# A two-layer hybrid trunk on one core: branch and output blocks as 512+256-column chains, with a written order on ScalarE and VectorE

## The chip, the cores and the metric

The kernel runs on one core of one Trainium2 chip. The metric is the device time of one execution in microseconds, the median of three runs: 999.44 us before (999.4 to 999.6). The profile is of one execution of the same program.

The engines are named as in the profile: PE is TensorE's matmuls and PEld its weight loads, DVE is VectorE, ACT is ScalarE, POOL is GpSimd, SP is SyncE, whose queue issues nearly all DMAs.

## The reference

Sequence 256, width 1024, two layers. All arithmetic is float32. One layer, cut to what matters:

```python
x = x + 0.5 * swiglu(rms_norm(x, ffn1_norm), ffn1_w_gate_up, ffn1_w_down)
z = rms_norm(x, mix_norm) @ w_in            # u (512), q, k, v (512 each), gate logits (2 x 1024)
y_pool = multiscale_pool(u, pool_w, pool_scale)     # trailing means over 2/4/8/16 positions
y_attn = moba_attention(rope(norm(q)), rope(norm(k)), v)   # one block of 256: causal attention
gates  = sigmoid(gl + b_gate)                       # 2 x 1024
merged = gates[0] * (y_pool @ w_branch_pool) + gates[1] * (y_attn @ w_branch_attn)
x = x + merged @ w_out
x = x + 0.5 * swiglu(rms_norm(x, ffn2_norm), ffn2_w_gate_up, ffn2_w_down)
```

## The kernel before

**Exact products from split operands.** Every float32 operand of a large matmul is held as two parts, high and low. A product of weights and activations is three terms: high weights by high activations, high by low, low by high. Activations lie as `[128, 2, 256]`: 256 columns of the high part, then 256 of the low part. `chain` (line 140) makes the three terms in two matmuls: the high weights against all 512 columns (both parts at once, into two halves of a PSUM tile), then the low weights against the 256 high columns, added to the first half. The two halves of the PSUM tile must be added afterwards. `chain3` (line 145) makes them in three matmuls of 256 columns, all into one half, so that nothing has to be added. Below, a *block* is one 128x128 weight block with its three terms; a *pair* is a block by `chain`, a *triple* a block by `chain3`.

**Weights.** They come in units of 16 blocks (1 MB): one DMA on SP into `raw` (four buffers), then for each of two halves a copy on ACT (`hi<-raw`, line 122) and a subtraction on DVE (`lo<-raw,hi`, line 123), each over 128x1024. `hi` and `lo` have six halves each, three units. `request` issues one unit's DMA and its two splits; `unit` takes the next one. `raw` comes free when DVE has made the low part, and only then can SP issue the DMA that waits for it.

**The order.** `mm` and whatever stands in `keep(...)` stays in the order in which it is written; the other instructions on ACT, DVE and POOL are placed among them by a list scheduler of the tile framework. Each engine runs its own list strictly in order.

**The stages of a layer.** FFN 1 (gate-up units, then down projection), then `mix`: q, k, v, u, the gates and attention interleaved, then the branch stage and the output stage, then FFN 2.

**Branch stage** (lines 737 to 780). For each of eight output blocks f there are 4 blocks of pooling (`pk`) and 4 of attention (`yk`): 64 blocks in a layer, four units. f = 2, 3 and 4 (`wide`) are pairs, whose halves are added by ACT and DVE (lines 756 and 757); the other five are triples. The first four f are done in two passes over k. `mixed(f)` multiplies by the two gates (line 758), adds the two products (line 759, on POOL for wide f) and splits the sum into `mk[f]` (`halves`: ACT line 205, DVE line 206).

**Output stage** (`project`, lines 783 to 804). For each f there are 8 blocks of `mk`: 64 in a layer, four units. f < 4 are pairs: ACT copies the second half to `t`, POOL adds x (line 799), DVE adds the first half (line 800). f >= 4 are triples with one addition on DVE. Then `after(f)`, which is `prep`: the new x is scaled and split into `hx[f]` for FFN 2 (ACT line 251, DVE line 252), squared and accumulated (lines 260 and 261).

**What waits there.** The output stage's first chains read `mk[0]` to `mk[5]` and only later `mk[6]`, `mk[7]`. FFN 2 begins with unit 0 over `hx[0]` to `hx[6]`, unit 1 over `hx[0]`, `hx[1]`, then `hx[7]`; after a few more blocks comes the sum of squares over the partitions, two matmuls `ss<-ar,one_r`, where `ar` is the split of `acc` and needs the last square.

Of the kernel before, what the change touches and what calls it, by code (L numbers as in the profile page):

```python
# [49 lines left out]
def trunk_kernel(ctx: ExitStack, tc: tile.TileContext, x_in, w_in, pw_in, qkn_in, rope_in, mask_in, band_in, out):  # L50
# [182 lines left out]
    nc.gpsimd.memset(uT[:, :, :PAD], 0.0)  # L233
# [8 lines left out]
    keep(nc.gpsimd.dma_start(gx[:, L * NG + 2 * S:L * NG + 4 * S], x_in[:, L * NG + 2 * S:L * NG + 4 * S]))  # L242

# [19 lines left out]
    def prep(f, l, col):  # L263
        split_x(f, l, col)
        square_x(f)
# [300 lines left out]
    def mix(l, after):  # L566
# [26 lines left out]
        def open_gate(f):  # L593
            tt(gates[:, f], gates[:, f], bc2(r), op=OP.mult)
            for j in range(2):
                c = j * NK + f
                act(gates[:, f, j, :], gates[:, f, j, :], AF.Tanh, scale=0.5, bias=hb[:, c:c + 1])
# [142 lines left out]
        def branch(f, j, k0=0, k1=4):  # L740
            if f not in sums:
                sums[f] = quarter("two")
            if f in wide:
                for k in range(k0, k1):
                    chain(sums[f][j], *ws[f // 2], f % 2 * 8 + j * 4 + k, (pk, yk)[j][k], k == 0, k == 3)
            else:
                chain3(sums[f][:, j], *ws[f // 2], f % 2 * 8 + j * 4 + k0, (pk, yk)[j][k0:k1], k0 == j == 0,
                       j == 1 and k1 == 4)

        def mixed(f):  # L750
            mg = tmp.tile([P, 2, S], F32, name="mg", tag="t512", bufs=5)
            both = sums[f]
            if f in wide:
                both = mg
                for i in range(2):
                    act(mg[:, i, :], sums[f][i][:, 1, :], AF.Copy)
                    tt(mg[:, i, :], sums[f][i][:, 0, :], mg[:, i, :], op=OP.add)
            stt(mg, gates[:, f], 1.0, both, op0=OP.add, op1=OP.mult)
            (nc.gpsimd.tensor_tensor if f in wide else tt)(mg[:, 0, :], mg[:, 0, :], mg[:, 1, :], op=OP.add)
            halves(mk[f], mg[:, 0, :])  # L760

        ws = [unit() for _ in range(2)]
        sums = {f: quarter("two") for f in range(2)}
        wide = range(2, 5)
        sums.update({f: banks(pmm, "two") for f in range(2, 4)})
        sums = {f: [z[:, j] for j in range(2)] if f in wide else z for f, z in sums.items()}
        sums[4] = [quarter("two") for _ in range(2)]
        for f in range(4):
            for j in range(2):
                branch(f, j, 0, 2)  # L770
        for f in range(4):
            for j in range(2):
                branch(f, j, 2)
            mixed(f)
        for f in range(4, NK):
            if f % 2 == 0:
                ws.append(unit())
            for j in range(2):
                branch(f, j)
            mixed(f)  # L780
        ws, sums = [], []

        def project(f, k0=0, k1=NK):
# [5 lines left out]
            if f >= 4:  # L789
                chain3(ps[:, 0], *ws[f // 2], f % 2 * 8 + k0, mk[k0:k1], k0 == 0, k1 == NK)  # L790
            else:
                for k in range(k0, k1):
                    chain(ps, *ws[f // 2], f % 2 * 8 + k, mk[k], k == 0, k == NK - 1)
            if k1 == NK:
                t = x[:, f, :]
                if f < 4:
                    t = small.tile([P, S], F32, name="t", tag="sg", bufs=2)
                    act(t, ps[:, 1, :], AF.Copy)
                    nc.gpsimd.tensor_tensor(t, t, x[:, f, :], op=OP.add)
# [135 lines left out]
```

## Time and profile before

| | |
|---|---|
| median of three runs | 999.44 us |
| profiled execution, its own time | 999.57 us |
| its span | 997.6 us |
| PE busy | 993.6 us, 100% of the span |
| DVE busy | 799.5 us, 80% |
| ACT busy | 628.7 us, 63% |
| POOL busy | 17.5 us, 2% |
| granted TensorE clock | 1.0 throughout |
| branch stage of layer 1, layer 2 | begins at 280.00 us and 774.11 us |
| output stage | begins at 301.90 us and 796.00 us |
| FFN 2 | begins at 323.59 us and 817.70 us |

A row of the timeline gives start, duration, engine, line, operation, tiles, shapes and count; equal instructions that follow each other are one row. The records of neighbouring instructions overlap: a matmul's record is longer than the distance to the next one's start. So rates are read from start to start. Groups give busy time, mean duration of one, and the idle time before them with what ended it.

### The profile page before, as it was taken

Reading aid. Unit: us, or ns where it says so; the run is one execution under the profiler, and the core shown is the slowest. Engines: PE = TensorE matmul, PEld = TensorE weight load, DVE = VectorE, ACT = ScalarE, POOL = GpSimd, SP = SyncE. Lnnn points to the kernel's source line nnn. Section 1 sums busy time; section 2 is a strip of 40 time slices with the busy share of each in tenths; the row PEclk is TensorE's granted clock in tenths of the full one; section 3 lists DMA queues with packets and bytes.
Section 4 is the critical chain, followed back from the end, with each engine's and each line's share of the span. In section 5 each row is a group of like instructions: output and inputs, shape, how many; then the busy total and the mean of one; then the engine's idle time right before and its main releaser. Section 6 shows DMA issues by size and latency. Waiting matters only on the chain.

```text
span 997.6 us, 15761 instructions
## 1 busy us (share of the span) xinstructions
PE 993.6 (100%) x6220; PEld 899.1 (90%) x6220; DVE 799.5 (80%) x1183; ACT 628.7 (63%) x999; POOL 17.5 (2%) x53
## 2 busy tenths in 40 slices
PE   9999999999999999999999999999999999999998
PEld 8998888898899988988898898888989999889888
DVE  7987786799879988886688888667998799888752
ACT  7766565657866766655576666556678567656541
POOL 1000000000001000000000000000000010000000
PEclk9999999999999999999999999999999999999999
DMA  9655565643536655655556566555545266555640
GB/s 314 243 207 209 194 245 214 220 170 120 219 127 211 214 208 182 204 207 204 181 193 215 178 211 205 182 204 191 193 151 194 100 235 216 198 204 189 211 143 27
DMA packets 30154, 192.88 MB, mean 193 GB/s; under 512 B 3360, under 2 KB 5408, under 8 KB 7552
## 3 DMA queue, kind: packets, MB, share of 16 engines
q1 hardware_dynamic: 29664, 191.18, 55.0%
q8 instruction: 48, 0.79, 0.3%
q0 software_dynamic: 128, 0.39, 0.1%
q10 hardware_dynamic: 288, 0.31, 0.1%
q14 instruction: 26, 0.21, 0.1%
HBM read 190.82 MB, written 1.05 MB: 192 GB/s over the span
## 4 chain that ended last, share of the span: by engine, by line
PE 100%; DVE 0%; issue 0%
PE ps L80 85%; PE pt L80 6%; PE two L80 4%; PE at L80 2%; PE pe L80 1%; PE at L546 1%; PE busy L80 0%; PE tp L507 0%; PE ss L80 0%; DVE gx L451 0%
## 5 line engine op out<-in xcount | busy, mean ns | idle before, releaser
L80 PE MATMUL ps<-hx,hi 128*128 128x512 f32 (+1 forms) x1714 | 572.2, 383 | 0.0
L123 DVE TENSOR_TENSOR lo<-raw,hi 128x1024 fp32r<-128x1024 f32 (+2 forms) x333 | 393.9, 1189 | 115.3 <-ACT hi L122 110.6
L80 PE MATMUL ps<-hx,lo 128*128 128x256 f32 x1712 | 464.6, 273 | 0.0
L122 ACT ACTIVATE hi<-raw 128x1024 fp32r<-128x1024 f32 (+2 forms) x333 | 339.6, 1029 | 190.4 <-PE ps L80 153.9
L80 PEld LDWEIGHTS ps<-hx,hi 128*128 128x128 f32 x1714 | 321.1, 188 | 56.8 <-issue 0.3
L80 PEld LDWEIGHTS ps<-hx,lo 128*128 128x128 f32 x1712 | 321.2, 188 | 0.8
L80 PE MATMUL ps<-ga,hi 128*128 128x512 f32 (+1 forms) x264 | 87.0, 376 | 0.0
L80 PE MATMUL ps<-gc,hi 128*128 128x512 f32 (+1 forms) x264 | 87.0, 376 | 0.0
L80 PE MATMUL ps<-ga,lo 128*128 128x256 f32 x256 | 69.9, 273 | 0.0
L80 PE MATMUL ps<-gc,lo 128*128 128x256 f32 x256 | 69.9, 273 | 0.0
L80 PE MATMUL ps<-gb,hi 128*128 128x512 f32 (+1 forms) x198 | 65.6, 376 | 0.0
L80 PE MATMUL pt<-hi,hx 128*128 128x512 f32 x192 | 64.3, 382 | 0.0
L80 PEld LDWEIGHTS ps<-ga,hi 128*128 128x128 f32 x264 | 49.0, 188 | 8.3
L80 PEld LDWEIGHTS ps<-gc,hi 128*128 128x128 f32 x264 | 49.0, 188 | 8.3
L80 PE MATMUL pt<-lo,hx 128*128 128x256 f32 x192 | 52.5, 273 | 0.0
L80 PE MATMUL ps<-gb,lo 128*128 128x256 f32 x192 | 52.4, 273 | 0.0
L190 DVE TENSOR_TENSOR ab<-ps,ab 128x512 f32<-128x512 f32 x56 | 38.6, 688 | 16.2 <-ACT ab L189 14.9
L80 PEld LDWEIGHTS ps<-ga,lo 128*128 128x128 f32 x256 | 48.1, 188 | 0.0
L80 PEld LDWEIGHTS ps<-gc,lo 128*128 128x128 f32 x256 | 48.1, 188 | 0.0
L388 DVE TENSOR_TENSOR lo<-raw,hi 128x1024 fp32r<-128x1024 f32 x38 | 44.7, 1217 | 0.0
L80 PE MATMUL two<-yp,hi 128*128 128x256 f32 (+1 forms) x208 | 43.9, 301 | 0.0
L80 PE MATMUL ps<-mk,hi 128*128 128x256 f32 (+1 forms) x192 | 43.5, 311 | 0.0
(162 smaller groups left out, 1130.1 us busy)
## 6 DMA issues: line engine op xcount, KB each, us to landing
raw<-w SPq DMA_DIRECT2D x176, 1024.0 KB, 4.9
raw<-w SPq DMA_DIRECT2D x6, 256.0 KB, 6.0
raw<-w SPq DMA_DIRECT2D x11, 128.0 KB, 3.8
raw<-w SPq DMA_DIRECT2D x2, 512.0 KB, 6.1
gx<-x SPq DMA_DIRECT2D x2, 256.0 KB, 5.7
qk<-pw SPq DMA_DIRECT2D x2, 256.0 KB, 3.3
out_dram<-gx SPq DMA_DIRECT2D x2, 256.0 KB, 2.7
out_dram<-gx SPq DMA_DIRECT2D x1, 384.0 KB, 5.4
```

Source lines behind the costliest of these rows:

```text
L80: return keep(nc.tensor.matmul(*args, **kw))
L122: put(act(hi, w, AF.Copy))
L123: put(tt(lo, w, hi.bitcast(F32), op=OP.subtract))
L190: put(tt(t, ps[:, :, 0, :], t, op=OP.add))
L388: keep(tt(lo[h], raw[:, h * HALF:(h + 1) * HALF], hi[h].bitcast(F32), op=OP.subtract))
L546: keep(nc.tensor.transpose(line(pt)[:, j * P:(j + 1) * P], pr[:, h, c * P:(c + 1) * P], ident))
```

## The change

- **Branch stage.** All eight f are pairs, one f after the other, each with its own PSUM tile (four single tiles by turns with the double ones). `mixed(f)` for each: two ACT copies, two additions, the gate product, the sum on DVE (none on POOL), `halves`. `mk[f - 1]` is split after f's gate product.
- **Gate 7.** Its sums are drained where they were, after three requests, but `open_gate(7)` (times r on DVE, two Tanh on ACT) stands behind f = 3.
- **Output stage.** All eight f are pairs: `t` copied by ACT, then two additions on DVE, none on POOL.
- **Weights.** `next_half` makes half a unit at a time at written places: after f = 0, 1, 2, 4 and 6 of the branches, three after the last, one after each of f = 0 to 5 of the output, two at the end.
- **Order.** All of these, and the `prep` behind the output stage, are in `keep`.
- **Padding.** The 16 zero columns of `uT` are cleared by 16 memsets of one column each, after POOL's DMA of x, in place of one memset before it.

```diff
-    nc.gpsimd.memset(uT[:, :, :PAD], 0.0)
...
     keep(nc.gpsimd.dma_start(gx[:, L * NG + 2 * S:L * NG + 4 * S], x_in[:, L * NG + 2 * S:L * NG + 4 * S]))
+    for t in range(PAD):
+        keep(nc.gpsimd.memset(uT[:, :, t:t + 1], 0.0))
...
-        gate(7)
-        open_gate(7)
+        last = sum_pair(unit())
+        for _ in range(3):
+            request()
+        drain(gates[:, 7], last, keep)
...
+        def next_half():
+            if not begun:
+                raw = raws.tile([P, 2 * HALF], F32, name="raw", tag="raw")
+                nc.sync.dma_start(raw, w_in[n_unit[0]])
+                n_unit[0] += 1
+                begun.append((raw, [], []))
+            raw, hi, lo = begun[0]
+            h = len(hi)
...
+            split(raw[:, h * HALF:(h + 1) * HALF], hi[h], lo[h], keep)
+            if h:
+                begun.clear()
+                ahead.append((hi, lo))
...
-            (nc.gpsimd.tensor_tensor if f in wide else tt)(mg[:, 0, :], mg[:, 0, :], mg[:, 1, :], op=OP.add)
-            halves(mk[f], mg[:, 0, :])
...
+        def mixed(f, ps):
+            mg = tmp.tile([P, 2, S], F32, name="mg", tag="t512", bufs=5)
             for j in range(2):
+                keep(act(mg[:, j, :], ps[j][:, 1, :], AF.Copy))
             for j in range(2):
+                keep(tt(mg[:, j, :], ps[j][:, 0, :], mg[:, j, :], op=OP.add))
+            keep(stt(mg, gates[:, f], 1.0, mg, op0=OP.add, op1=OP.mult))
+            return mg
...
+        for f in range(NK):
             if f % 2 == 0:
                 ws.append(unit())
+                ps = [quarter("two") for _ in range(2)]
+            else:
+                ps = banks(pmm, "two")
+                ps = [ps[:, j] for j in range(2)]
             for j in range(2):
+                for k in range(4):
+                    chain(ps[j], *ws[f // 2], f % 2 * 8 + j * 4 + k, (pk, yk)[j][k], k == 0, k == 3)
+            mgs.append(mixed(f, ps))
+            if f:
+                halves(mk[f - 1], mgs[f - 1][:, 0, :], keep)
+            keep(tt(mgs[f][:, 0, :], mgs[f][:, 0, :], mgs[f][:, 1, :], op=OP.add))
+            if f == 3:
+                open_gate(7, keep)
+            if f in (0, 1, 2, 4, 6):
+                next_half()
+        halves(mk[-1], mgs[-1][:, 0, :], keep)
+        for _ in range(3):
+            next_half()
...
-            if f >= 4:
-                chain3(ps[:, 0], *ws[f // 2], f % 2 * 8 + k0, mk[k0:k1], k0 == 0, k1 == NK)
...
             if k1 == NK:
-                    nc.gpsimd.tensor_tensor(t, t, x[:, f, :], op=OP.add)
-                tt(x[:, f, :], ps[:, 0, :], t, op=OP.add)
+                t = small.tile([P, S], F32, name="t", tag="sg", bufs=2)
+                keep(act(t, ps[:, 1, :], AF.Copy))
+                keep(tt(x[:, f, :], ps[:, 0, :], x[:, f, :], op=OP.add))
+                keep(tt(x[:, f, :], x[:, f, :], t, op=OP.add))
+                if f < 6:
+                    next_half()
                 after(f)
...
+        for _ in range(2):
+            next_half()
```

ACT's list in layer 1, from the drain of gate 7 to the copy for f = 4 (`gates<-gates,hb` is the Tanh, `mg<-two` the copy of a wide sum's second half), before:

```order
L189 ACTIVATE gates<-ps 128x512
L597 ACTIVATE gates<-gates,hb 128x256 x2
L122 ACTIVATE hi<-raw 128x1024
L205 ACTIVATE mk<-mg 128x256
L122 ACTIVATE hi<-raw 128x1024 x2
L756 ACTIVATE mg<-two 128x256
```

ACT's list in the change, from the copies for f = 2 to those for f = 4:

```order
L764 ACTIVATE mg<-two 128x256 x2
L205 ACTIVATE mk<-mg 128x256
L122 ACTIVATE hi<-raw 128x1024
L764 ACTIVATE mg<-two 128x256 x2
L205 ACTIVATE mk<-mg 128x256
L598 ACTIVATE gates<-gates,hb 128x256 x2
L764 ACTIVATE mg<-two 128x256 x2
```

The two Tanh of gate 7 moved from ahead of the branches to between the copies for f = 3 and f = 4.

DVE's list in layer 1 for one f of the branch stage and the gate product that follows f = 3, before (f = 1 and 2, as the scheduler mixed them):

```order
L758 SCALAR_TENSOR_TENSOR mg<-gates,two 128x512
L123 TENSOR_TENSOR lo<-raw,hi 128x1024
L759 TENSOR_TENSOR mg<-mg 128x256
L757 TENSOR_TENSOR mg<-two,mg 128x256
L123 TENSOR_TENSOR lo<-raw,hi 128x1024
L206 TENSOR_TENSOR mk<-mg,mk 128x256
```

DVE's list in the change, f = 3 and the beginning of f = 4:

```order
L766 TENSOR_TENSOR mg<-two,mg 128x256 x2
L767 SCALAR_TENSOR_TENSOR mg<-gates,mg 128x512
L206 TENSOR_TENSOR mk<-mg,mk 128x256
L784 TENSOR_TENSOR mg<-mg 128x256
L595 TENSOR_TENSOR gates<-gates,r 128x512
L766 TENSOR_TENSOR mg<-two,mg 128x256 x2
L767 SCALAR_TENSOR_TENSOR mg<-gates,mg 128x512
```

Every f has now two additions `mg<-two,mg`, and the sum `mg<-mg` is always DVE's.

DVE's list in layer 1 at the end of the output stage (`gx` holds x), f = 4 and 5 before:

```order
L800 TENSOR_TENSOR gx<-ps,gx 128x256 x2
L123 TENSOR_TENSOR lo<-raw,hi 128x1024
L252 SCALAR_TENSOR_TENSOR hx<-gx,hx 128x256
L261 TENSOR_TENSOR acc<-acc,sq 128x256
L252 SCALAR_TENSOR_TENSOR hx<-gx,hx 128x256
L261 TENSOR_TENSOR acc<-acc,sq 128x256
```

The same place in the change, f = 4 and the beginning of f = 5:

```order
L805 TENSOR_TENSOR gx<-ps,gx 128x256
L806 TENSOR_TENSOR gx<-gx,t 128x256
L123 TENSOR_TENSOR lo<-raw,hi 128x1024
L253 SCALAR_TENSOR_TENSOR hx<-gx,hx 128x256
L262 TENSOR_TENSOR acc<-acc,sq 128x256
L805 TENSOR_TENSOR gx<-ps,gx 128x256
L806 TENSOR_TENSOR gx<-gx,t 128x256
```

Each f has one more addition, and half a weight unit stands between the new x and its split in each f up to 5.

More of the change, by code (lines that the diff above doesn't have):

```diff
@@ L591, in gate, with open_gate @@
             pair(unit(), gates[:, f], *other)
[L593 to L594 removed]
+        def open_gate(f, put=lambda i: i):
+            put(tt(gates[:, f], gates[:, f], bc2(r), op=OP.mult))
             for j in range(2):
                 c = j * NK + f
[L597 removed]
+                put(act(gates[:, f, j, :], gates[:, f, j, :], AF.Tanh, scale=0.5, bias=hb[:, c:c + 1]))
         def project_u():
@@ L734, in mix @@
             map_end(2 + p, ats[2 + p])
-        gate(7)
-        open_gate(7)
+        last = sum_pair(unit())
+        for _ in range(3):
+            request()
+        drain(gates[:, 7], last, keep)
         mt = acts.tile([P, NK, 2, S], F32R, name="mk", tag="ga")
         mk = [mt[:, i] for i in range(NK)]
[L740 to L748, printed above, removed]
@@ L750, in mixed @@
-        def mixed(f):
-            mg = tmp.tile([P, 2, S], F32, name="mg", tag="t512", bufs=5)
[L752 to L759, printed above, removed]
-            halves(mk[f], mg[:, 0, :])
@@ L762, in mix @@
[L762 to L768, printed above, removed]
+        begun = []
+        def next_half():
[6 more added lines that the diff above has]
+            h = len(hi)
+            hi.append(parts.tile([P, HALF], F32R, name="hi", tag="hi"))
+            lo.append(parts.tile([P, HALF], F32R, name="lo", tag="lo"))
+            split(raw[:, h * HALF:(h + 1) * HALF], hi[h], lo[h], keep)
+            if h:
+                begun.clear()
+                ahead.append((hi, lo))
@@ L788, in project @@
             ps = sums[f]
-            if f >= 4:
-                chain3(ps[:, 0], *ws[f // 2], f % 2 * 8 + k0, mk[k0:k1], k0 == 0, k1 == NK)
-            else:
-                for k in range(k0, k1):
-                    chain(ps, *ws[f // 2], f % 2 * 8 + k, mk[k], k == 0, k == NK - 1)
-            if k1 == NK:
[L795 to L799, printed above, removed]
-                tt(x[:, f, :], ps[:, 0, :], t, op=OP.add)
+            for k in range(k0, k1):
+                chain(ps, *ws[f // 2], f % 2 * 8 + k, mk[k], k == 0, k == NK - 1)
+            if k1 == NK:
+                t = small.tile([P, S], F32, name="t", tag="sg", bufs=2)
[4 more added lines that the diff above has]
+                    next_half()
                 after(f)
@@ L839, in trunk_kernel @@
                 keep(nc.sync.dma_start(d, z))
-        mix(l, lambda f: prep(f, l, C_G2))
+        mix(l, lambda f: prep(f, l, C_G2, keep))
         if l + 1 < L:
```

14 lines of the change are left out of this document (4 added, 10 removed).

## The prediction

> **What bounds the kernel now.** The engine shares and the chain of waits come first.
>
> ```profile
> PE 993.6 (100%) x6220; PEld 899.1 (90%) x6220; DVE 799.5 (80%) x1183; ACT 628.7 (63%) x999; POOL 17.5 (2%) x53
> ...
> PE 100%; DVE 0%; issue 0%
> ```
>
> PE never waits, and nothing but PE is on the chain. So the time is the sum of the matmuls' distances, and a change can do two things: alter that sum, or make PE wait for the first time. For the first, the timeline of PE around the two stages of layer 1 (layer 2 repeats it 494.1 us later):
>
> ```profile
> 280.00 0.39 PE L80 MATMUL two<-yp,hi 128*128 128x256 f32 x2
> ...
> 280.35 0.39 PE L80 MATMUL two<-yp,hi 128*128 128x256 f32 x2
> ...
> 301.90 0.39 PE L80 MATMUL ps<-mk,hi 128*128 128x512 f32 x1
> ...
> 323.59 0.38 PE L80 MATMUL ps<-hx,hi 128*128 128x512 f32 x1
> ...
> 331.59 0.39 PE L80 MATMUL ss<-ar,one_r 128*128 128x256 f32 x2
> ...
> 440.18 0.38 PE L80 MATMUL ps<-hx,hi 128*128 128x512 f32 x1
> ...
> 446.51 0.38 PE L80 MATMUL ps<-gb,hi 128*128 128x512 f32 x1
> ```
>
> From 440.18 to 446.51 lie 19 pairs: 0.333 us each. A triple takes 0.345 (280.00 to 280.35). The 128 blocks of both stages take 323.59 - 280.00 = 43.59 us.
>
> For the second, DVE in stretches of the same layer (columns: stretch, length, then busy time and count of PE, PEld, DVE, ACT, POOL, granted clock, DMA share and rate):
>
> ```profile
> 280.00:286.00 6.00, 6.00 (x48) 5.73 (x47) 2.52 (x3) 2.46 (x4) 0.00 (x0) 1.00 0.46 149
> ...
> 310.00:316.00 6.00, 6.00 (x47) 5.73 (x46) 5.10 (x7) 5.09 (x11) 4.25 (x4) 1.00 0.64 205
> 316.00:324.00 8.00, 8.00 (x71) 7.97 (x70) 8.00 (x18) 5.79 (x11) 0.55 (x1) 1.00 0.64 236
> 324.00:330.00 6.00, 6.00 (x38) 5.40 (x38) 6.00 (x10) 3.96 (x7) 0.00 (x0) 1.00 0.62 194
> ```
>
> DVE is idle early in the branch stage, but from 316 to 330 us it is busy without a gap. The 80% of the page hide that: at the end of `mix` DVE has no reserve, and just there the change gives it more to do.
>
> **The change on PE.** It takes triples away: 5 of 8 f in the branches, 4 of 8 in the output stage. 128 pairs of 0.333 us are 42.67 us; less 43.59 is -0.92 us a layer, -1.84 us in both. That is the whole gain, and it is had only if PE still never waits.
>
> **The change on DVE.** Durations and distances, in groups by form and in the timeline:
>
> ```profile
> L757 DVE TENSOR_TENSOR mg<-two,mg 128x256 f32<-128x256 f32 x12 | 4.7, 415 | 0.1
> ...
> 296.47 1.28 DVE L758 SCALAR_TENSOR_TENSOR mg<-gates,mg 128x512 f32<-128x512 f32 x2
> ...
> 316.76 0.41 DVE L261 TENSOR_TENSOR acc<-acc,sq 128x256 f32<-128x256 f32 x1
> 317.09 0.75 DVE L800 TENSOR_TENSOR gx<-ps,t 128x256 f32<-128x256 f32 x2
> 317.76 1.21 DVE L123 TENSOR_TENSOR lo<-raw,hi 128x1024 fp32r<-128x1024 f32 x1
> 318.89 0.47 DVE L252 SCALAR_TENSOR_TENSOR hx<-gx,hx 128x256 fp32r<-128x256 f32 x1
> 319.29 0.41 DVE L261 TENSOR_TENSOR acc<-acc,sq 128x256 f32<-128x256 f32 x1
> ...
> 282.32 0.68 DVE L190 TENSOR_TENSOR gates<-ps,gates 128x512 f32<-128x512 f32 x1
> ...
> 443.50 0.68 DVE L190 TENSOR_TENSOR ab<-ps,ab 128x512 f32<-128x512 f32 x1
> 444.22 0.69 DVE L341 TENSOR_TENSOR ab<-ab,r 128x512 f32<-128x512 f32 x1
> ```
>
> From start to start: an operation over 256 elements 0.333 us (three from 316.76 to 317.76), a low part 1.13 (to 318.89), a split of `hx` 0.40, one over 512 elements 0.60 (1.28 less one of 0.68). An operation that needs the result just before it starts 0.04 after that one's end (444.22), not 0.08 before: 0.45 in place of 0.333 for a short one.
>
> I add up DVE's list from the first branch's addition to the low part of `ar`, as the change writes it:
>
> - Eight branch blocks: additions 0.333 + 0.45 (the gate product waits for the second), gate product 0.60, split of `mk` and sum 0.333 each: 2.05, together 16.4.
> - 16 low parts (five among the branches, three after them, six in the output, two at its end): 18.1.
> - The product for gate 7, moved here: 0.6.
> - Eight output blocks: 0.45 for the first addition (the second waits for it), 0.333, `hx` 0.40, and 0.333 for seven of the squares: 11.8.
> - One drain of FFN 2 (0.6) and `ar` (0.4): 1.0.
>
> Sum 47.9 us without a wait. The list begins at about 282.9: PE is through with the first branch at 280.00 + 8 x 0.333 = 282.67, and DVE drains gate 7 from 282.32 on (row above), as the change leaves it. PE, without waits, comes to the second matmul of `ss`, which needs this `ar`, at 331.59 + 0.11 - 0.92 = 330.8, that is 47.9 us later. **So DVE has exactly as much work as PE in this stretch, and each wait of DVE becomes one of PE.** DVE does wait, for ACT:
>
> ```profile
> 283.76 0.91 ACT L597 ACTIVATE gates<-gates,hb 128x256 f32<-128x256 f32 x2 [2.13 <-DVE gates L594]
> ...
> L122 ACT ACTIVATE hi<-raw 128x1024 fp32r<-128x1024 f32 x316 | 332.2, 1058 | 189.4 <-PE ps L80 153.9 <-PE pt L80 11.8 <-issue 8.5
> L251 ACT ACTIVATE hx<-gx 128x256 fp32r<-128x256 f32 x47 | 23.3, 499 | 11.1 <-DVE gx L800 9.5 <-DMA gx<-x 1.7
> L205 ACT ACTIVATE mk<-mg 128x256 fp32r<-128x256 f32 x16 | 6.7, 416 | 10.3 <-DVE mg L759 7.6 <-POOL mg L759 2.7
> L756 ACT ACTIVATE mg<-two 128x256 f32<-128x256 f32 x12 | 3.8, 374 | 0.0
> ```
>
> - *Gate 7.* The Tanh stand ahead of the copies for f = 4 on ACT, and wait for DVE's product, which stands behind f = 3. DVE gets there at 282.9 + 2.85 (f = 0, no `mk` yet, with a low part) + 2 x 3.18 (f = 1 and 2, each with a low part) + 2.05 + 0.6 + 0.2 = 295.0; f = 4's sums have been done since 280.00 + 5 x 2.67 = 293.3. ACT then does two Tanh (0.91) and a copy (0.37, begun 0.1 early), and DVE, whose next instruction is f = 4's addition, waits 1.25 with 0.07 for the two handovers.
> - *The last `mk`.* Nothing else stands between the last sum and its split: 0.42 + 0.06 of waiting, and while DVE splits (0.42) ACT makes the next high part (1.06): another 0.55.
> - *The ends of the output stage.* f = 6 and 7 have no weights between the new x and its split: ACT's 0.50 and 0.06, twice. After the last square DVE waits 0.45 for ACT's next high part, 1.06 long.
> - A copy of f = 1: 0.2.
>
> Together 4.0 us; the eight instructions ahead of such waits also lose their overlap of 0.08: 0.6. DVE is done at 282.9 + 47.9 + 4.6 = 335.4, and PE does the second `ss` matmul at 335.45 in place of 331.7: **+3.75 us a layer**, which is 4.67 us of waits less the 0.92 saved. PE should meet them first at the output stage, where k = 5 of its first chain (301.33 + 5 x 0.333 = 303.0) finds `mk[5]` not yet split, then in FFN 2 at `hx[5]`, `hx[6]` and `hx[7]`, and at `ar`. After that FFN 2 goes at the old rate; nothing in it gives PE's time back.
>
> **What costs nothing.** POOL's work that moves to DVE (three sums, four additions) is in the counts above. So is what its absence gives:
>
> ```profile
> 313.95 2.59 POOL L799 TENSOR_TENSOR t<-t,gx 128x256 f32<-128x256 f32 x2 [1.67 <-ACT t L798]
> ...
> 314.19 1.76 DVE L123 TENSOR_TENSOR lo<-raw,hi 128x1024 fp32r<-128x1024 f32 x1
> 315.88 0.95 DVE L252 SCALAR_TENSOR_TENSOR hx<-gx,hx 128x256 fp32r<-128x256 f32 x1
> ```
>
> While POOL added, these two took 1.76 and 0.95 us, and 1.21 and 0.47 without it (rows above): 1.0 us a layer that goes. I have taken the undisturbed durations; were the long ones DVE's own, the sum would be 2 us higher. The Trainium skill, "SBUF — State Buffer", section "Who interferes with whom", says that a DVE instruction with two SBUF inputs contends with a GpSimd instruction that reads SBUF, which is what these rows show; by it the lower sum holds.
>
> The padding (a piece of the chain in order of time, then POOL's timeline):
>
> ```profile
> 28.80 153.34 PE ps L80 x920
> ...
> 2.08 0.17 POOL L233 MEMSET uT<- 128x64 f32 x1
> ...
> 2.69 0.58 POOL L238 MEMSET inv<- 128x1 f32 x15
> ...
> 3.56 0.57 POOL L242 DMA_DIRECT2D gx<-x  x1
> ```
>
> Sixteen such memsets take some 0.6 us, at about 4 us, and `uT` is first used in `mix`, behind FFN 1, whose matmuls run to 182 us (28.80 + 153.34); the DMA goes out 0.08 us earlier. Nothing, and 0.6 us if nothing covered it. SP's DMAs stay one per unit, and wait for low parts that DVE makes later; three units lie ready ahead of the stage, so I take nothing for them, and price the other case as a rival. The new copies on ACT (ten of 0.37 in the branches, four in the output, some 5 us a layer) find it idle for 2.2 us from 316 to 324 and 2.0 from 324 to 330, more than the stage's share of them; where they hold DVE up they are counted.
>
> **The sum.** 999.57 (profiled execution) + 2 x 3.75 = 1007.1; from the median, 999.44 + 7.5 = 1006.9. DVE's distances are read to 0.01 us over some 110 instructions in the stretch; those roundings, and small waits between dependent instructions that I left out, go rather up than down. I say **1007.2 us**. A DVE 2% faster or slower than the sum is 1 us a layer, 2 us in all; half of the waits filled is -4. Own range 1004 to 1010.
>
> **Rivals.**
>
> *PE never waits.* Then 999.57 - 1.84 = 997.7 us, no more than the same. It holds if DVE's list to `ar` takes 47.9 us with its waits, against my 52.5. For it: PE meets no wait now, and DVE idles 3.5 us from 280 to 286. Against it: that idle time lies ahead of the first branch's sums and cannot be used, and 316 to 330 is full already.
>
> *Half of it.* ACT gets to the copies for f = 4 and to the splits at the end sooner than I reckon, because PE's own waits give DVE nothing to do for less time: about 2 us a layer, 1003.4 us. Against it: ACT and DVE run their lists in order, and the price of each wait is a row.
>
> *Weights late too.* DVE is behind by 4.7 us at `ss`, nearly two units of low parts (2 x 1.13 each). If FFN 2 finds its units not split, each unit costs up to 2.3 us: 1007.1 + 2 x 2.3 = 1011.7. Against it: the low parts of FFN 2's first two units stand ahead of `ar` in the list and are in the sum.
>
> *The clock.* If PE's clock falls with the waits, the 8 us from FFN 2's beginning to `ss` at half rate would be up to 16, less the waits already there: up to +3.5 a layer, 1014. The granted clock is 1.00 in each stretch shown, none of which holds a wait of PE. The Trainium skill, "TensorE: Matmul & The Clock Gate", section "HAM oscillation — how this bites in real kernels", has the clock halved after some 3.4 us without work; no trace here shows such a gap. By that rule it stays, since my 4.7 us are spread over six operands.
>
> **How the numbers follow.** Forecast 0.80, half 0.08, no wait 0.05, weights late 0.05, clock 0.02. The range takes in half the waits and a DVE some 2% slower with rounding up: 1003.4 to 1010.5. Below 0.2% (2 us) a time cannot be told from the old one. Only "no wait" can be within it, at -0.18%: same 0.04, faster 0.01, slower 0.95.
>
> **What would show it.** Right: pairs of 0.333 in both stages; DVE without a gap from about 297 to 335 but for the waits named, ACT's Tanh row ahead of the copies for f = 4 with an idle time before it of some 3 us; PE's first waits at `ps<-mk` (DVE `mk`), then at `ps<-hx` and `ss` (DVE `hx`, `ar`), 4 to 5 us a layer, and nowhere else; FFN 2 after `ss` as long as before. Wrong: PE at 100% again, or waits in the branch stage itself, in FFN 2 for `lo`, or a lower clock.

## The result

The changed kernel took **1013.26 us** (median of six runs) against 999.54 in the same comparison: a ratio of 1.0137, 95% interval 1.0114 to 1.0160. The prediction was 1007.2 us, with a range of 1003.4 to 1010.5. Its direction was right and its time was not.

The six runs stand in three groups: 1008.62 and 1009.00; 1013.23 and 1013.29; 1017.82 and 1017.87. They lie about 4.5 us apart, and only the lowest group is inside the range. So there are two things to explain: why the lowest group is 9 us above the kernel before, and where the steps come from. The profiled run is of the upper group (1017.87 us, span 1016.0).

### The profile page after: what moved, and what is told of

It reads as the page before. It is cut to its first block, busy times and chain, and to the rows that moved or that the text cites. A ratio compares the mean times of both kernels' runs of the same rounds, so it can differ in the third digit from the quotient of the medians.

```text
span 1016.0 us, 15537 instructions
## 1 busy us (share of the span) xinstructions
PE 1005.8 (99%) x6076; PEld 896.9 (88%) x6076; DVE 814.4 (80%) x1225; ACT 635.8 (63%) x1027; POOL 3.5 (0%) x54
## 4 chain that ended last, share of the span: by engine, by line
PE 90%; DVE 8%; ACT 1%; issue 1%; DVEq 0%
PE ps L80 79%; PE pt L80 6%; DVE lo L123 3%; PE at L80 1%; PE two L80 1%; DVE mg L766 1%; DVE mg L767 1%; DVE hx L253 1%; DVE gx L805 1%; PE pe L80 1%; PE at L547 1%; DVE mg L784 1%; DVE gx L806 0%; DVE acc L262 0%; ACT hi L122 0%
## 5 line engine op out<-in xcount | busy, mean ns | idle before, releaser
L80 PE MATMUL ps<-hx,hi 128*128 128x512 f32 (+1 forms) x1714 | 580.9, 386 | 3.0 <-DVE hx L253 3.0
L80 PE MATMUL ps<-mk,hi 128*128 128x512 f32 x128 | 43.6, 386 | 1.2 <-DVE mk L206 1.2
L80 PE MATMUL two<-yp,hi 128*128 128x512 f32 x128 | 42.8, 382 | 0.0
```

The source lines that it names most:

```text
L80: return keep(nc.tensor.matmul(*args, **kw))
```

## The profile after

The engine shares and the chain of waits of the changed kernel:

```profile
PE 1005.8 (99%) x6076; PEld 896.9 (88%) x6076; DVE 814.4 (80%) x1225; ACT 635.8 (63%) x1027; POOL 3.5 (0%) x54
...
PE 90%; DVE 8%; ACT 1%; issue 1%; DVEq 0%
```

PE has 144 matmuls fewer than before and yet 12 us more busy time. Of the chain, 8% has gone to DVE. Cut the span where the branch stage begins and where the pairs go on behind `ss`. PE's timeline of the changed kernel, and then the rows of the kernel before at the same places (its layer 1 begins the branches at 280.00, a row in the prediction):

```profile
280.23 0.38 PE L80 MATMUL two<-yp,hi 128*128 128x512 f32 x1
...
336.49 0.39 PE L80 MATMUL ps<-hx,hi 128*128 128x512 f32 x1
...
783.50 0.38 PE L80 MATMUL two<-yp,hi 128*128 128x512 f32 x1
...
839.70 0.40 PE L80 MATMUL ps<-hx,hi 128*128 128x512 f32 x1
```

```profile
331.82 0.39 PE L80 MATMUL ps<-hx,hi 128*128 128x512 f32 x1
...
774.11 0.39 PE L80 MATMUL two<-yp,hi 128*128 128x256 f32 x2
...
825.93 0.39 PE L80 MATMUL ps<-hx,hi 128*128 128x512 f32 x1
```

| stretch | before, us | after, us | more |
|---|---|---|---|
| start to the branches of layer 1 | 280.00 | 280.23 | .23 |
| layer 1, branches to behind `ss` | 51.82 | 56.26 | 4.44 |
| behind `ss` to the branches of layer 2 | 442.29 | 447.01 | 4.72 |
| layer 2, branches to behind `ss` | 51.82 | 56.20 | 4.38 |
| behind `ss` to the end of the span (997.6, 1016.0) | 171.67 | 176.30 | 4.63 |

The 18.4 us come in two nearly equal halves. The stretches that the change rewrote cost 8.8 us more, where the prediction said 7.5. The other 9.35 us lie in FFN 2 and what follows it, whose matmuls the change leaves as they were (.23 us lie ahead of the branches; their cause is shown in the last section).

**The first half: PE's waits.** They are clearest in a second trace of the changed kernel (the run "after_again" below), whose clock stayed at 1.00. PE in layer 1; the brackets hold the idle time before the row and what ended it:

```profile
304.60 0.49 PE L80 MATMUL ps<-mk,hi 128*128 128x512 f32 x1 [0.58 <-DVE mk L206]
...
328.35 0.48 PE L80 MATMUL ps<-hx,hi 128*128 128x512 f32 x1 [0.49 <-DVE hx L253]
...
330.54 0.50 PE L80 MATMUL ps<-hx,hi 128*128 128x512 f32 x1 [1.25 <-DVE hx L253]
...
335.20 0.38 PE L80 MATMUL ss<-ar,one_r 128*128 128x256 f32 x1 [0.20 <-ACT ar L205]
336.80 0.38 PE L80 MATMUL ss<-ar,one_r 128*128 128x256 f32 x1 [1.21 <-DVE ar L206]
```

They stand at the operands that the prediction named (`mk`, `hx`, `ar`; the two `hx` are f = 5 and 6, and at `hx[7]` PE lost only .15 us). Behind each wait the first pair takes .10 to .12 us longer. Why DVE is late shows in its own timeline in the profiled run:

```profile
296.85 0.76 DVE L766 TENSOR_TENSOR mg<-two,mg 128x256 f32<-128x256 f32 x2 [1.25 <-ACT mg L764]
...
317.30 0.42 DVE L805 TENSOR_TENSOR gx<-ps,gx 128x256 f32<-128x256 f32 x1
...
319.96 0.41 DVE L805 TENSOR_TENSOR gx<-ps,gx 128x256 f32<-128x256 f32 x1
...
329.40 0.48 DVE L253 SCALAR_TENSOR_TENSOR hx<-gx,hx 128x256 fp32r<-128x256 f32 x1 [0.58 <-ACT hx L252]
...
331.59 0.48 DVE L253 SCALAR_TENSOR_TENSOR hx<-gx,hx 128x256 fp32r<-128x256 f32 x1 [0.58 <-ACT hx L252]
...
332.85 2.36 DVE L123 TENSOR_TENSOR lo<-raw,hi 128x1024 fp32r<-128x1024 f32 x2 [0.43 <-ACT hi L122]
```

The stall behind gate 7's Tanh (1.25 us), the two at the last `hx` (.58 each) and the one behind the last square (.43) are there within .02 us of the forecast. The rows at 317.30 and 319.96 are the same addition for two blocks that follow each other: DVE needs 2.66 us for an output block with its half unit of weights. PE needs 8 x .333 = 2.67. In the output stage DVE can therefore not regain what it has lost earlier.

**The second half: another rhythm.** The view by stretches of time, over 100 us in the middle of FFN 2 of each layer, where PE never waits (columns as in the prediction: stretch, length, busy time and count of PE, PEld, DVE, ACT, POOL, granted clock, DMA share and rate). Before:

```profile
340.00:440.00 100.00, 100.00 (x602) 89.96 (x601) 84.59 (x117) 64.01 (x99) 0.00 (x0) 1.00 0.57 196
845.00:945.00 100.00, 100.00 (x602) 89.99 (x602) 83.25 (x113) 62.53 (x94) 0.00 (x0) 1.00 0.56 194
```

After:

```profile
340.00:440.00 100.00, 100.00 (x586) 88.39 (x585) 83.43 (x116) 63.22 (x96) 0.00 (x0) 1.00 0.58 200
845.00:945.00 100.00, 100.00 (x587) 88.37 (x585) 82.96 (x115) 62.83 (x95) 0.00 (x0) 1.00 0.57 196
```

PE counts as busy 100 us in all four rows and the clock is 1.00 in all four, but 586 matmuls go through in place of 602. That is 2.7% slower: 342 ns a pair in place of 333. Sixteen of 602 over some 170 us is 4.5 us, one step between the groups. In layer 1 it lasts until 519 us, just behind the next `ss`; in layer 2 to the end. In layer 2 it had also run through the output stage: behind the wait for `mk`, from 807.27 to 830.65 us, PE's 67 pairs took 342 ns each. That changed nothing in the time, because PE waits for DVE at the end of that stretch in any case; the wait at the first `hx` is missing there instead.

**The clock.** It did fall once in the profiled run:

```profile
326.00:330.00 4.00, 2.25 (x13) 1.53 (x11) 3.39 (x8) 2.17 (x6) 0.00 (x0) 1.00 0.43 117
330.00:334.00 4.00, 4.00 (x14) 3.43 (x15) 2.95 (x7) 2.71 (x4) 0.00 (x0) 0.57 0.38 158
```

A mean of .57 over 4 us is half speed for about 3.4 of them, behind two waits of .49 and 1.26 us. It cost next to nothing, because DVE had not yet made `ar`: the wait at `ss` shrank to .28 us, from 1.21 in the second trace. The stretch to behind `ss` took 56.26 us with the fall and 56.20 (layer 2) without it. The runs agree: the fastest of the six, 1008.62 us, has a mean clock of .996, about what two such stretches would give (an estimate, 2 x 3.4 x .5 of 1007 us).

## The experiments

Theory A: DVE's full list makes PE wait (some 9 us in all), and a wait can put PE's stream of pairs into a slower rhythm, which then stays. Rivals: the slow rhythm belongs to the new order of the work, to a full DVE, or to the clock.

### after_again: the same kernel once more

> The changed kernel itself, for the spread of its times and a second trace. Theory A (a wait of TensorE can put the stream of pairs into a slower rhythm, 342 ns a pair in place of 333, which then stays for one FFN 2, about 504 pairs by 9 ns or 4.5 us, in each layer or not): the times fall into three groups, about 1008.8, 1013.3 and 1017.8 us, and in the trace of a run of the middle group exactly one of the two layers has its pairs at 342 ns behind `ss`; of a run of the lowest group, none. Theory B (the slow rhythm belongs to the new order of the work and is always there, and the groups come from the granted clock or something else): both layers at 342 ns in every trace, and the groups differ by clock or by the length of the waits.

Measured: 1008.64, 1009.01, 1009.13, 1009.60, 1013.39 and 1013.61 us. The profiled run is one of the middle group (1013.61):

```profile
340.00:440.00 100.00, 100.00 (x602) 89.97 (x601) 85.47 (x119) 64.75 (x97) 0.00 (x0) 1.00 0.60 202
845.00:945.00 100.00, 100.00 (x587) 88.39 (x586) 82.42 (x114) 61.29 (x94) 0.00 (x0) 1.00 0.56 192
```

One layer in the quick rhythm, one in the slow one, at the same clock and behind the same waits: .20 and 1.21 us at `ss` in layer 1 (rows above), .20 and 1.22 in layer 2. The same program goes either way, so B falls. Counted by their times (none, one or two slow layers for the three groups), the twelve runs of both comparisons took the slow rhythm in 8 of 24 layers.

### second_ss: two matmuls that wait for nothing

```diff
             columns(ws[1], pss[1], range(4, NK))
+            factor_sums(ars[-1])
```

> The changed kernel with the two matmuls of `ss` issued a second time, 4 steps of columns behind the first, into another bank and read by nobody; their operands are long ready, so TensorE waits for nothing there. It comes in both FFN 2 and in the second FFN 1; three times two matmuls at .115 us are +.7 us. In the trace of the changed kernel the slow rhythm of layer 1 ended some pairs behind the next `ss`, which had not waited. Theory A1 (two 256-column matmuls without a wait bring the fast rhythm back): all runs at 1008.8 + .7 + at most .3, so 1009.5 to 1010, and pairs at 333 ns soon behind the second `ss`. Rival A2 (the end of the rhythm there was chance, or had to do with the stage): three groups again, 1009.5, 1014 and 1018.5 us.

Measured: 1009.59, 1009.59, 1009.65, 1009.73, 1009.75 us. The groups are gone. The two stretches of its trace:

```profile
340.00:440.00 100.00, 100.00 (x602) 90.00 (x601) 85.56 (x119) 64.85 (x98) 0.00 (x0) 1.00 0.59 203
845.00:945.00 100.00, 100.00 (x602) 89.94 (x601) 84.81 (x117) 63.10 (x96) 0.00 (x0) 1.00 0.57 193
```

In layer 1 the pairs behind the first `ss` (which waited) went at 341 ns, and at 333 from the first pair behind the second. A1 holds: two matmuls of 256 columns that do not wait bring the quick rhythm back. They cost .7 us (1009.65 against 1009.0, the mean of the six runs of the lowest group), and the mean of the changed kernel's twelve runs, 1011.9, falls by 2.3. In this profiled run (1009.59) the clock fell at the same place as in the first trace (its mean is .998), and its time is that of the others.

With the groups gone, 1009.65 is a firm base for taking the first half apart. The next four carry the second `ss`, too.

### gate7_early

```diff
         drain(gates[:, 7], last, keep)
+        open_gate(7, keep)
...
-            if f == 3:
-                open_gate(7, keep)
```

> The changed kernel with the second `ss` (which held all runs at 1009.65), and the gate of block 7 opened right behind its drain, ahead of the branches, in place of behind block 3. Prediction's step (the Tanh of gate 7 stops VectorE 1.25 us a layer and TensorE pays all of it): 1009.65 - 2.5 = 1007.2 us. Rival (VectorE's list is as long as before, only the stall is gone, and the instructions behind it wait for TensorE's sums instead): above 1008.7 us.

Measured: 1009.52 us (1009.28 to 1009.71). No gain; but the test did not do what I wanted. DVE's row of this trace:

```profile
285.33 0.76 DVE L770 TENSOR_TENSOR mg<-two,mg 128x256 f32<-128x256 f32 x2 [1.25 <-ACT mg L768]
```

The stall is still 1.25 us long, only at 285.33 in place of 296.85: ACT does the two Tanh just ahead of another block's copies. It was moved, not removed, and in this other place it leaves the time as it was. What it costs is not shown by this run.

### branches_only and outputs_only: each half alone

For the branches alone, the output of the changed kernel goes back to what it was:

```diff
+            if f >= 4:
+                chain3(ps[:, 0], *ws[f // 2], f % 2 * 8 + k0, mk[k0:k1], k0 == 0, k1 == NK)
...
+                    keep(nc.gpsimd.tensor_tensor(t, t, x[:, f, :], op=OP.add))
-                keep(tt(x[:, f, :], x[:, f, :], t, op=OP.add))
```

> One half of the change alone, with the second `ss`: branch blocks in pairs in the written order, but output blocks as before (f < 4 in pairs with GpSimd adding t and x, f >= 4 in three matmuls with one addition of VectorE). TensorE does .37 us a layer more than in the changed kernel, VectorE has 8 additions of .42 us less a layer (3.4 us). Theory (VectorE's list sets the waits, us for us): 1009.65 - 2 x (3.4 - .37) = 1003.6 us, up to 1004.6 if GpSimd's additions slow VectorE. Rival (the branches alone make the waits, and the output's additions fit between): 1009.65 + .7 = 1010.4 us.

For the outputs alone, the kernel before gets the change's two additions and eight chains:

```diff
-            if f >= 4:
-                chain3(ps[:, 0], *ws[f // 2], f % 2 * 8 + k0, mk[k0:k1], k0 == 0, k1 == NK)
...
-                    nc.gpsimd.tensor_tensor(t, t, x[:, f, :], op=OP.add)
-                tt(x[:, f, :], ps[:, 0, :], t, op=OP.add)
+                tt(x[:, f, :], ps[:, 0, :], x[:, f, :], op=OP.add)
+                tt(x[:, f, :], x[:, f, :], t, op=OP.add)
```

> The other half of the change alone, with the second `ss` (+.7 us): the kernel before with all output blocks in pairs and both of a block's additions on VectorE, branches as before, VectorE's order left to the scheduler. TensorE has 32 triples less a layer (-.37 us), VectorE 8 additions of .42 us more (3.4 us), GpSimd 4 less. Theory (what a layer's list of VectorE gains, TensorE waits, beyond the .83 us that `ar` was early): 999.5 + .7 + 2 x (3.4 - .83 - .37) = 1004.6 us. Rival (VectorE has room in the output stage as long as the branches do not fill it first, and only both halves together overfill it): 999.5 + .7 - .7 = 999.5, up to 1000.5 us.

Measured: the branches alone 1005.27 us (1005.06 to 1005.85), between the theory and its rival. The outputs alone 1000.73 (1000.51 to 1001.50, and one of twelve at 1005.09): the rival. Without the .7 us of the second `ss` the branches alone cost about 4.8 us over the kernel before, the outputs .2, and both together 9. They do not add. The outputs alone leave DVE's list just short of full: in their trace `ar` is ready some .5 us ahead of the matmul that reads it (DVE ends it at 331.63, PE wants it at 332.12), where it was .95 us in the kernel before. Behind branches that fill the list first, the same additions are waited for.

### triples_late: a dose of DVE alone

```diff
+            if f >= 4:
+                chain3(ps[:, 0], *ws[f // 2], f % 2 * 8 + k0, mk[k0:k1], k0 == 0, k1 == NK)
...
+                if f < 4:
                     keep(tt(x[:, f, :], x[:, f, :], t, op=OP.add))
```

> The changed kernel with the second `ss`, and the output blocks f >= 4 in three matmuls as before: one addition of VectorE (.333 us from start to start, .42 us long) and one copy of ScalarE less for each of the four, and no GpSimd, so nothing slows VectorE. TensorE does .37 us a layer more. Theory (TensorE waits for VectorE's list us for us): 1009.65 - 2 x (4 x .333 - .37) = 1007.7 us, 1007.0 with .42. Rival (the list's end is set by ScalarE, whose copies come between, and each block that goes back takes VectorE's wait for that copy away too): 1009.65 - 2 x (4 x (.333 + .37) - .37) = 1004.8 us. Rival (the waits at `hx[7]` and `ar` come from what stands behind the last sum, whatever the list before): 1009.65 + .7 = 1010.4 us.

Measured: 1005.83 us (1005.55 to 1006.19), between the theory and the first rival. Its DVE timeline shows why; the first additions of three blocks that follow each other, f = 3 with a second addition behind it and f = 4 without:

```profile
320.34 0.42 DVE L812 TENSOR_TENSOR gx<-ps,gx 128x256 f32<-128x256 f32 x1
...
323.00 0.41 DVE L812 TENSOR_TENSOR gx<-ps,gx 128x256 f32<-128x256 f32 x1
...
325.20 0.42 DVE L812 TENSOR_TENSOR gx<-ps,gx 128x256 f32<-128x256 f32 x1
```

A pair's block takes DVE 2.66 us, a triple's 2.20: .46 less, not .333, since the second addition also makes the first wait for its result. Four blocks are 1.84 us a layer. I had also taken off PE's .37 us for the triples. That was wrong: PE waits for DVE at the end of this stretch, so its own work does not show in the sum. With both put right it is 1009.65 - 2 x 1.84 = 1006.0 us, which is worked out after the result.

### wait_at_ss: a wait without anything else

```diff
+        if late_on[0]:
+            al = acts.tile([P, 2, 2, S], F32R, name="late", tag="tok", bufs=2)[:, 0, 0]
+            for _ in range(4):
+                keep(nc.gpsimd.tensor_copy(al, ar[:, 1, :].bitcast(F32)))
```

> The kernel before, with one thing added: in FFN 2 the second matmul of `ss` takes the remainder of `ar` from a copy that GpSimd makes four times over. The branches and outputs are as before, VectorE has nothing more to do. In the trace of before `ar` is ready .83 us ahead of `ss`; four copies at .84 us (GpSimd's addition of this size, an estimate) make TensorE wait about 2.5 us in each layer (1.5 if a copy takes .6). Theory A (a wait of TensorE at `ss` by itself sets the slow rhythm): 999.5 + 5 us of waits, and 0, 4.5 or 9 us more, in runs that differ by such steps; pairs at 342 ns behind `ss` in a trace of an upper group. Rival B (the rhythm comes from the new forms and order of branches and outputs, or from a full VectorE): 999.5 + 5 = 1004.5 us (1002.5 with the faster copies) in every run, pairs at 333 ns behind `ss`.

Measured: 1003.32, 1003.39, 1003.77, 1003.89, 1003.92, and 1006.95 us. PE waited 1.66 us in each layer, and the pairs behind it went at 333 ns in this trace:

```profile
334.19 0.38 PE L80 MATMUL ss<-late,one_r 128*128 128x256 f32 x1 [1.66 <-POOL late L294]
```

Five of six runs fit B. The one at 1006.95 lies 3.3 us higher, less than a whole step, and has no trace. By itself this run speaks against A, or for a smaller chance of the slow rhythm than I thought.

### wait_on_pair: the wait in front of a pair

```diff
+                for _ in range(4):
+                    keep(nc.gpsimd.tensor_copy(late[:, 0], ar[:, 1, :].bitcast(F32)))
+                keep(nc.gpsimd.tensor_copy(late, hk[NK - 1].bitcast(F32)))
+                for j in range(2):
+                    chain(pss[1][:, j], *ws[1], 2 * NK - 2 + j, late, False, True)
```

> The kernel before, with a wait of TensorE put into the stream of pairs behind `ss`: in FFN 2 the second unit's last two pairs take `hx[7]` from a copy that GpSimd makes late (four copies of `ar` first, which took 2.66 us in the run with the wait at `ss`, then `hx[7]`, 512 columns, about 1.3 us as an estimate from twice .665). `ar` comes near 330.8, the copy near 334.9 to 335.3, and the pairs want it near 334.0: a wait of about 1.1 us in each layer. Branches, outputs and VectorE's work are as before. Theory A (behind a wait in front of a pair the stream starts in the fast or in the slow rhythm by chance, and stays in it until an `ss` that does not wait): 999.5 + 2 x 1.2 = 1002 us in the lowest runs, others 4.5 or 9 us above them, and in a trace of such a run pairs at 342 ns from the wait to the end of that FFN 2. Rival B (a wait alone is not enough, the branches and outputs in pairs or a full VectorE must come before it): all runs within .5 us of 1002, pairs at 333 ns.

Measured: ten runs from 1000.20 to 1000.89 us, and two at 1004.63 and 1005.93. The profiled one is that at 1005.93. PE waited less than planned, .22 us a layer, since the copy of 512 columns took .61 us where I had estimated 1.3, and it waited equally long in both:

```profile
334.53 0.49 PE L80 MATMUL ps<-late,hi 128*128 128x512 f32 x1 [0.22 <-POOL late L346]
...
834.21 0.49 PE L80 MATMUL ps<-late,hi 128*128 128x512 f32 x1 [0.22 <-POOL late L346]
...
340.00:440.00 100.00, 100.00 (x586) 88.39 (x585) 82.11 (x113) 61.87 (x96) 0.00 (x0) 1.00 0.57 197
845.00:945.00 100.00, 100.00 (x603) 90.01 (x602) 83.81 (x113) 62.41 (x94) 0.00 (x0) 1.00 0.58 200
```

In layer 1 the slow rhythm begins with the pair at 334.53 and ends at 515, behind the next `ss`: 527 pairs at 342.5 ns. In layer 2 the pairs go on at 333. Branches, outputs and DVE's work are those of the kernel before. So the slow rhythm can begin with the very pair that waited, after .22 us and without the rest of the change: A holds, with a smaller chance here (2 of 24 layers, counted by the times) than in the changed kernel. That a wait is not the only thing behind which it begins is shown in the last section.

### relieved, no_waits, no_waits_2, no_waits_3: pairs without the waits

The first gives DVE less to do and `ss` a later place:

```diff
+            if f % 2:
+                drain(mg, ps, keep)
...
+            keep((nc.gpsimd.tensor_tensor if f < 7 else tt)(mgs[f][:, 0, :], mgs[f][:, 0, :], mgs[f][:, 1, :], op=OP.add))
...
-            for u, k0, k1 in ((0, 0, NK - 1), (1, 0, 2), (0, NK - 1, NK), (1, 2, 4)):
+            for u, k0, k1 in ((0, 0, NK - 1), (1, 0, 4), (0, NK - 1, NK), (1, 4, 6)):
```

> The changed kernel with VectorE relieved and TensorE given other work ahead of its waits: gate 7 opened right behind its drain, odd branch blocks drained 512 wide by one instruction of each engine, the addition of the two halves of `mg` on GpSimd for f < 7, output blocks f >= 4 in three matmuls as before (no ScalarE copy, one VectorE addition less), and `ss` two steps of columns later. All branch blocks stay in pairs. VectorE's list between the first branch addition and `ar` is shorter by 7 x .42 (additions to GpSimd), 4 x .25 (one instruction for two), 4 x .42 (the triples) = 5.6 us, which is more than the 4.0 us that TensorE waited in a layer by my count; the triples cost TensorE .37 us a layer against the changed kernel, the later `ss` covers 1.33 us. Theory (VectorE's list is what TensorE waited for, and the slow rhythm needs a wait): no wait of TensorE over .3 us, the fast rhythm throughout, 999.5 - 2 x .46 = 998.6 us, up to 1000.5 if GpSimd's additions slow VectorE as they did in the trace of before (`lo` 1.76 in place of 1.21 us). Rival (the new order costs by itself, waits or not): above 1004 us.

Measured: 1001.70 and 1002.06 us, and five runs from 1006.06 to 1006.94. Neither 998.6 nor above 1004 throughout. PE still waits, .19 (layer 1) and .35 us (layer 2) at `hx`, and most at a new place: FFN 2's third unit finds the first one's sums not drained, since the later `ss` also made unit 0 end later.

```profile
335.88 0.48 PE L80 MATMUL ps<-hx,hi 128*128 128x512 f32 x1 [0.89 <-DVE hold L190]
...
831.17 0.48 PE L80 MATMUL ps<-hx,hi 128*128 128x512 f32 x1 [0.88 <-DVE hold L190]
...
340.00:440.00 100.00, 100.00 (x603) 89.98 (x602) 85.25 (x119) 63.92 (x98) 0.00 (x0) 1.00 0.58 200
845.00:945.00 100.00, 100.00 (x587) 88.40 (x586) 81.71 (x112) 61.15 (x92) 0.00 (x0) 1.00 0.56 194
```

Again two waits alike, .89 and .88 us, and two rhythms. In this kernel the wait comes behind `ss`, so nothing resets the rhythm before the next `ss`.

The next one moves the first drain of FFN 2 ahead of the next unit's split and makes `ar` earlier:

```diff
-        for _ in range(2):
-            next_half()
+        next_half()
+        ars.append(factor_parts(keep))
+        next_half()
...
+            for u, k0, k1 in ((0, 0, 6), (1, 0, 2), (0, 6, NK), (1, 2, 5)):
...
+            drain(ts[0], pss[0], put)
...
+        request((), put)
```

> The version relieved once more: as the run so called, but only three of the additions of `mg` on GpSimd (f = 4, 5, 6), `ss` at the place of its operands (`ar` made between the two halves of the last split, ahead of the first drain of FFN 2, its two matmuls 26 pairs into FFN 2), unit 0 of FFN 2 taken to step 6, two steps of unit 1, then the rest of unit 0, so that `hx[6]` and `hx[7]` are wanted 16 and 18 pairs in (they were ready 3.9 and 5.7 us into the stage in the relieved run), and the first drain of FFN 2 placed ahead of the next unit's split on ScalarE and VectorE (in the relieved run TensorE waited .88 us a layer for it). Theory (waits of TensorE for VectorE are all that the pairs cost): no waits over .2 us, 999.5 - 2 x .46 (40 triples of a layer's branches turned into pairs at .0115 us) = 998.6 us and no run in an upper group. Rival (a list this full always leaves a wait somewhere): 1000 to 1002 us, and some runs 4.5 us above that.

Measured: 999.57 us median, ten runs from 999.12 to 999.74, and one at 1008.59, two steps higher: between the theory and its rival. PE still lost .34 us to a wait for `mk` in layer 1 and .2 at `hx[7]` in each layer, the slower restart included. The last two differ from it by one step of unit 1, and from each other by the additions on GpSimd:

```diff
-            for u, k0, k1 in ((0, 0, 6), (1, 0, 2), (0, 6, NK), (1, 2, 5)):
+            for u, k0, k1 in ((0, 0, 6), (1, 0, 3), (0, 6, NK), (1, 3, 6)):
```

> As the run without waits, with what its trace still showed mended: all additions of `mg` but the last on GpSimd again (behind three of seven, TensorE waited .34 us for `mk` in layer 1; in the relieved run, with seven, nothing), and three steps of unit 1 ahead of the rest of unit 0 in FFN 2, in place of two, so that `hx[7]` is wanted 20 pairs in instead of 18 (it was .2 us late in both layers). Theory: no wait, 999.5 - 2 x .46 = 998.6 us. Rival (what the pairs save is given back elsewhere, by GpSimd's additions slowing VectorE or by a wait at the next place in the list): 999.2 us or more.

> As no_waits_2, with three additions of `mg` on GpSimd (f = 4, 5, 6) in place of seven. Against it this tells what GpSimd's additions cost. Theory: the wait of .34 us for `mk` in one layer stays, the one for `hx[7]` goes: 999.5 - .9 + .3 = 998.9 us. Rival (GpSimd's additions cost more than they free): below no_waits_2.

Measured: with seven additions on GpSimd 998.49 us (998.18 to 998.99, and one of eleven at 1003.27), with three 998.63 (998.47 to 999.21); before 999.85. The forecasts were 998.6 and 998.9; neither rival came. The ratios are .9991 (.9983 to 1.0000) and .9988 (.9979 to .9996). The last one's page:

```profile
PE 992.8 (100%) x6140; PEld 895.5 (90%) x6140; DVE 807.1 (81%) x1203; ACT 632.5 (63%) x1011; POOL 9.0 (1%) x60
```

PE is busy .8 us less than before (993.6), and the time falls by 1.2. All branch blocks are pairs (the output blocks f >= 4 stay triples), and the kernel takes 1.2 us less than the one before, about .1%, and 14.6 less than the median of the changed one. Where the additions run makes no difference that these runs resolve.

## Why the prediction was right or wrong

- **PE's own work, -0.92 us a layer: right in layer 1.** The branch stage took 64 x .333 = 21.33 us (280.23 to 301.56), and the output stage's pairs went at .333 between the waits. In layer 2 the output stage went at .342, hidden by the waits behind it.
- **DVE's list is as long as PE's stretch: right**, with its waits, their places and their sizes. Gate 7 was 1.25 predicted and 1.25 measured, `hx` .56 and .58 each, the end .45 and .43. The seven waits of layer 1 sum to 4.04 us, where I had 4.0; with the short ones between dependent operations DVE idles 4.6, as forecast.
- **The sum of the waits, +3.75 us a layer: too small by .6.** PE did the second matmul of `ss` 56.04 us behind the first branch (280.23 to 336.27), where I had 55.45 (280.00 to 335.45). The operations themselves were 1% short. DVE in layer 1, from the first branch's addition to the low part of `ar` (stretch, length, busy time and count, clock, DMA share and rate):

```profile
283.14:336.23 53.09, 48.46 (x91) 0.97 0.46 160
```

  The list is busy for 48.46 us, where I had added up 47.9 (the row counts 91 operations, not some 110). I had said that the roundings go up rather than down, and did not put it into the sum. Two layers at 4.4 us are 8.8 of the 9.1 us by which the lowest runs lie above the kernel before.
- **"After that FFN 2 goes at the old rate": the step that failed.** I took PE's rate behind a wait from a trace in which PE does not wait. The wait ended and the slower rhythm stayed, 4.5 us a layer in a third of the layers. This, not the size of the waits, carried the median out of the range. How many layers a set of runs catches is chance: the median of after_again, the same kernel, is 1009.36 us, inside the range. The timeline of the kernel before did hold the rhythm, behind the triples of its branches:

```profile
288.18 0.38 PE L80 MATMUL two<-yp,hi 128*128 128x512 f32 x1
...
293.65 0.39 PE L80 MATMUL two<-yp,hi 128*128 128x256 f32 x2
```

  Between these rows lie 16 pairs, 342 ns each, and PE does not wait there. I took 333 ns from one long stretch alone.
- **The clock, at 0.02: the fall came, its price did not.** My reason against it (the waits are spread, no long gap) was wrong: the clock fell behind two waits of .49 and 1.26 us, in two of the six places where the traces have such a pair of waits. The Trainium skill, "TensorE: Matmul & The Clock Gate", section "HAM oscillation — how this bites in real kernels", speaks of idle gaps of more than some 3.4 us; this trace does not agree, with 1.26 us as its longest. The price was nearly nothing because the half-speed stretch lay inside a wait for DVE.
- **GpSimd's cost to DVE, 1.0 us a layer for the output's four additions: right to leave out.** In the changed kernel, where GpSimd adds nothing, all 16 low parts of this stretch take 1.22 to 1.23 us. By the dose of triples_late, branches_only should have gained 8 x .46 = 3.7 us a layer and gained 2.2. Its trace, with GpSimd's additions back, shows where such time goes:

```profile
315.28 0.42 DVE L814 TENSOR_TENSOR gx<-ps,t 128x256 f32<-128x256 f32 x1 [0.63 <-POOL t L813]
...
317.15 0.97 DVE L263 TENSOR_TENSOR acc<-acc,sq 128x256 f32<-128x256 f32 x1
...
319.90 0.96 DVE L263 TENSOR_TENSOR acc<-acc,sq 128x256 f32<-128x256 f32 x1
...
322.65 0.41 DVE L263 TENSOR_TENSOR acc<-acc,sq 128x256 f32<-128x256 f32 x1
```

  DVE waits .63 us for a sum of GpSimd's, and beside GpSimd two additions to `acc` take .97 and .96 us in place of .41, and one low part 1.76 in place of 1.22. These are 2.3 us, more than the 1.5 that are missing, so the account is not closed to better than .8 us. The padding's memsets had no run of their own.

## What to carry to other kernels

When PE is at 100% and another engine is nearly full in one stage, compare that stage's work per block on both (here 2.66 us on DVE and 2.67 on PE): what adds .46 us a block to DVE there comes back as PE's waiting, and an edit that is free alone can be dear behind another. Count matmuls over a fixed stretch, not busy time, before and behind the first wait: a wait's price may go on after it has ended. Take the waits away by moving what is wanted early (the order of units, the place of a drain) before taking work away.

## What was not expected of the hardware

- **A stream of 512+256-column pairs has two rhythms**, 333 and 342 ns, at the same granted clock (1.00). Behind a wait of .2 to 1.3 us (once behind one of .07, for `mk` in no_waits) it starts in either one, by chance, and stays there for up to 527 pairs (180 us). With the second `ss`, one of 32 runs in five kernels stood a step high (1005.09), so 1 layer of 64; in the changed kernel without it, 8 of 24. Of 81 runs of the kernel before, in which PE does not wait, three stood 4 us high (1003.55, 1003.48 and 1003.47) and one 2 us (1001.60); none of these has a trace.
- **The slow rhythm needs no wait.** The first 24 pairs of `mix`, up to its `ss`, have the operands the other way round (`pt<-hi,hx`), and PE does not wait there in any trace. Seventeen of them before, and then the same ones in the changed kernel (FFN 1, which ends there, is the same in both):

```profile
183.69 0.38 PE L80 MATMUL pt<-hi,hx 128*128 128x512 f32 x1
...
189.36 0.38 PE L80 MATMUL pt<-hi,hx 128*128 128x512 f32 x1
```

```profile
183.74 0.39 PE L80 MATMUL pt<-hi,hx 128*128 128x512 f32 x1
...
189.56 0.39 PE L80 MATMUL pt<-hi,hx 128*128 128x512 f32 x1
```

  That is 333 and 342 ns a pair. In the fourteen traces of all these kernels the stretch is slow in layer 1 in eleven and in layer 2 in three, and each time the pairs behind the `ss` that follows go at 333. Of the .23 us by which the changed kernel comes later to its first branch, .17 lie here. Between the triples of the old branches (the rows at 288.18 and 293.65) the pairs are slow in all eight stretches of the four traces that have them. So the rhythm can change where the stream of pairs is broken or its kind of matmul changes, and a wait of PE is one such place among others; that taking away the waits takes away the steps is therefore shown only as a smaller chance (one of the 22 runs of no_waits_2 and no_waits_3 stood a step high).
- **What is open:** why there are two rhythms. Neither clock, nor waits, nor the order of work tells them apart in the records. Why a wait in front of the pairs alone (2 of 24) and at the second matmul of `ss` alone (at most 1 of 12) was a rarer trigger than the changed kernel's series (8 of 24) was not settled either; with three high runs of the kernel before, the untraced one of the two high runs of wait_on_pair may have come without its wait. That it was the two short matmuls in a row, rather than any break in the pairs, that resets it was not tried apart; the triples of the old branches are short matmuls in a row, too, and the pairs behind them start slow.
- **The clock halved for 3.4 us behind waits of .49 and 1.26 us** in layer 1 of two traces (the changed kernel, second_ss), and not behind the same two waits in layer 2 of second_ss, in either layer of after_again, nor in layer 1 of gate7_early. In layer 2 of the changed kernel the first of the two waits is missing, and the clock stayed.
